# Input projections by Strassen block products over pairs of 512-token blocks, context tokens apart

## The chip, the cores and the metric

The kernel runs on one core of a Trainium2 chip. The metric is the device time of one execution, in microseconds (us); lower is better. Engines are named as in the profile: PE multiplies matrices (PEld is its weight load, which overlaps it), DVE, ACT and POOL work on vectors, SP only issues transfers. Work on one engine runs in the order in which it is written; between engines semaphores order it.

## The reference

One layer of a diffusion backbone: 2048 latent tokens of width 1024 and 256 context tokens.

```python
hx = modulate(rmsnorm(x, g_norm1[l]), mx[0], mx[1])      # (2048, 1024)
hc = modulate(rmsnorm(ctx, g_norm1[l]), mc[0], mc[1])    # (256, 1024)
px = split(hx @ w_in[l], IN_SPLIT_IDX)    # q 512, k 128, v 128, hq 512, i 512, ff 512, fb 512, g 512
pc = split(hc @ w_in[l], IN_SPLIT_IDX)
...
att_x = latent_attention(qx, kx, vx, kc, vc)             # softmax, 8 query heads, 2 key heads
hg_x, hg_c = hgrn2_bidirectional(px[3:], pc[3:], ...)    # gated recurrence over hq, i, ff/fb, g
x = x + mx[2] * (concat([att_x, hg_x]) @ w_out[l])
x = x + mx[5] * swiglu(modulate(rmsnorm(x, g_norm2[l]), mx[3], mx[4]), w_gu[l], w_down[l])
```

The change concerns the products of `hx` and `hc` with `w_in`. Of the context tokens only k, v, i and the two f are needed. All of it is float32.

## The kernel before

Float32 products are made of rounded parts: a factor is split into a high part (an ACT copy into a type with fewer bits) and a low part (the exact rest, one subtraction), and a product is high x high + high x low + low x high. So each product is three matmuls per 128 rows of the inner dimension.

The stages of the core's span, in order: an opening that loads the first columns of `w_mod` and the first tokens; normalisation, transposition and splitting of the tokens into `hT[b]` (block 0 is the context, blocks 1 to 4 are 512 latent tokens each), beside which PE already runs `jobs_kv` and the first half of hq; then the input projections, one after the other: q, the second half of hq, g, f and i; then attention and recurrence, the output projection, and the feed-forward part, which already uses Strassen's seven products.

The stretch that the change rewrites is q to i. A step is 256 columns of `w_in`, loaded into `wst` (1 MB), split by `split_w` (ACT copy L218, four DVE subtractions of 128x512 at L221) one step ahead into one of two homes, and then used for all tokens:
- "rows" jobs (`jobs_q`, `jobs_g`, `jobs_i`, by `mm_rows`, L442 and L448) give a tile of 128 tokens by 256 columns: for each of the 8 slices of 128 of the inner dimension a matmul of 512 columns (high tokens against high and low weights side by side) and one of 256 (low tokens against high weights). `both` (L453, L454) adds the two halves of the PSUM bank;
- "cols" jobs (`jobs_hq`, `jobs_f`, by `mm_cols`, L435) give a tile of 128 columns by 512 tokens (256 for the context): 24 matmuls, weights stationary.

The context's share of f and i is the first tiles of their steps. Behind the tiles, `pump` advances generators of side work: `qk_side` (normalisation and rotation of q and k, which are written to DRAM and read again; its transpositions are PE's), `mod_chunk` (16 products with further columns of `w_mod`, on DVE, L415 and L417) and, in the last step, `first_maxima` (the first row maxima of attention). PE's order here is written by hand; the order on the other engines is set by a list scheduler that knows a cost for each instruction, and SP issues nearly all transfers in one order too.

Of the kernel before, what the change touches and what calls it, by code (L numbers as in the profile page):

```python
# [9 lines left out]
F32 = mybir.dt.float32  # L10
# [57 lines left out]
def block_kernel(ctx: ExitStack, tc: tile.TileContext, a: dict, out: bass.AP, dbg=None):  # L68
# [24 lines left out]
    s_m0 = dram("s_m0", [4, P])  # L93
    s_att = [dram(f"s_att{j}", [256, T]) for j in range(2)]
# [79 lines left out]
    def load_tokens(gr, home, sp):  # L174
# [3 lines left out]
        for j in range(2):  # L178
            xt = home.tile([P, D], F32, tag="xt", name=f"xt{gr}_{j}")
            last_x[0] = nc.sync.dma_start(xt, src[j * P:(j + 1) * P, :])  # L180
            jk = xp2.tile([P, D], F32, tag="jk", name=f"jk{gr}_{j}") if gr else None
            xs.append((xt, jk))
# [21 lines left out]
    def load_raw(i, pieces):  # L204

        ws = wst_p.tile([P, KT, 256], F32, tag="wst", name=f"ws{i}")
# [7 lines left out]
    def split_w(i, ws, wp):  # L214

        whl = wp.tile([P, KT, 2, 256], F32R, tag="wh", name=f"wh{i}")
        wh, wl = whl[:, :, 0, :], whl[:, :, 1, :]
        nc.scalar.activation(wh, ws, AF.Copy)  # L218
        for q in range(4):
            ks = slice(2 * q, 2 * q + 2)  # L220
            (nc.vector if q % 2 or i > 1 else nc.gpsimd).tensor_tensor(  # L221
                wl[:, ks, :], ws[:, ks, :], f32v(wh[:, ks, :]), op=ALU.subtract)
        return wh, wl, whl
# [85 lines left out]
    with proj as st:  # L309
        w_pools = [w_left, w_right]  # L310
        hTp = pool(st, "hT")
        ev = pool(st, "ev", NEV)
        sm = pool(st, "sm", 4)
        sizes = [256, 512, 512, 512, 512]
        hT = [None] * 5
        for b in (4, 3, 1, 2):
            hT[b] = [hTp.tile([P, KT, sizes[b]], F32R, name=f"hT{w}{b}") for w in "hl"]
        ps_mm = pool(st, "ps_mm", 4, PSUM)
        nchunk = [1]
        turned = [None]  # L320

        def load_w(pieces):
# [3 lines left out]
            return split_w(i, load_raw(i, pieces), w_pools[i % 2])  # L326

        first = [early_w]
        with ExitStack() as p1:
            ps_x = pool(p1, "ps_x", 4, PSUM)  # L330
            xh = pool(p1, "xh", 3)
            for gr in list(range(1, NTOK // 256)) + [0]:
                if gr == 0:
                    xp.close()
                    hTc = pool(st, "hTc", side="right")
                    hT[0] = [hTc.tile([P, KT, 256], F32R, name=f"hT{w}0") for w in "hl"]
                    xp2 = pool(p1, "xp3", 2, side="right")
# [6 lines left out]
                with behind:  # L344
                    if gr == 1:
                        xs = early_x
                    else:
                        xs = ahead if gr == 2 else load_tokens(gr, xpp if gr else xp2, sm)
                        if gr == 0:
                            xs = [(xt, hT[0][1][:, 4 * j:4 * j + 4, :].rearrange("p k t -> p (k t)"))  # L350
                                  for j, (xt, _) in enumerate(xs)]
# [27 lines left out]
                def split_h(kk, hv, eng):  # L379

                    hi = hT[b][0][:, 2 * kk:2 * kk + 2, o:o + 256]
                    hd = nc.scalar.activation(hi, hv, AF.Copy)
                    return hd, eng.tensor_tensor(hT[b][1][:, 2 * kk:2 * kk + 2, o:o + 256], hv, f32v(hi), op=ALU.subtract)
# [11 lines left out]

        evF = pool(st, "evF", 1, side="right")
        qp = pool(st, "qp", 1, side="right")
        ps_t = pool(st, "ps_t", 2, PSUM)
        ps_q = pool(st, "ps_q", 2, PSUM)
# [30 lines left out]
        def mm_cols(pm, w, b, c0):  # L430

            n = sizes[b]
            for k in range(KT):
                for i, (wi, hi) in enumerate(((0, 0), (0, 1), (1, 0))):
                    nc.tensor.matmul(pm[:, :n], w[wi][:, k, c0:c0 + P], hT[b][hi][:, k, :],  # L435
                                     start=(k == 0 and i == 0), stop=(k == KT - 1 and i == 2))

        def mm_rows(pm, w, b, j, t=None):

            js = slice(j * P, (j + 1) * P)  # L440
            for k in range(KT):
                first = nc.tensor.matmul(pm, hT[b][0][:, k, js], w[2][:, k, :, :].rearrange("p w c -> p (w c)"),  # L442
# [1763 lines left out]
```

## Time and profile before

| | |
|---|---|
| median of 3 runs | 3110.43 us (3109.83 to 3116.51) |
| profiled execution | 3117.9 us, of it span 3116.1 us |
| granted clock | 0.996 |
| opening | 0 to 41 us |
| tokens, kv, first half of hq | 41 to 152 us |
| q, second half of hq | 152 to 292 us |
| g, f, i | 292 to 710 us |
| attention, recurrence, output projection | 710 to 1823 us |
| feed-forward | 1823 to 3116 us |

The stage borders are the first and last starts of each tile's matmuls in the trace. Tables by window give, for a stretch of the span, how long each engine was busy in it, with the number of its instructions in brackets; the timeline gives single instructions with their start, their length, and the idle time ahead of them with what ended it. The length of a matmul in the timeline includes its way through the pipeline; the rate is the distance between starts.

### The profile page before, as it was taken

The numbers are of one execution on the slowest core, as the hardware profiler recorded it, in microseconds if no ns is written. First come the engines' busy times: TensorE is split into PE (matmuls) and PEld (weight loads), VectorE is DVE, ScalarE is ACT, GpSimd is POOL, SyncE is SP. The second block draws the span as 40 slices with busy tenths as digits, with TensorE's granted clock in tenths as the row PEclk, the third lists the DMA queues.
The fourth block names the chain that finished last, engine by engine and source line by source line (L and its number), as shares of the span: only waits on it lengthen the run. The fifth ranks groups of instructions, "written<-read, shape, count | busy, mean of one in ns | idle before, by whom it ended". The sixth has DMA issues, their size and how long they took to land.

```text
span 3116.1 us, 51235 instructions
## 1 busy us (share of the span) xinstructions
PE 3074.8 (99%) x18844; PEld 2483.8 (80%) x18844; DVE 1845.9 (59%) x3252; ACT 1303.1 (42%) x2656; POOL 1602.7 (51%) x1291
## 2 busy tenths in 40 slices
PE   9999999999999999999999999999999999999999
PEld 7888888886777778777778878788888788888887
DVE  4554655427777787786745574544478743333567
ACT  4422322214545545555553253333345533333454
POOL 3311212106989888898862118676600277776122
PEclk9999999999999999999999999999999999999999
DMA  7544544425111212111124444656596533333765
GB/s 244 159 139 127 155 139 150 141 69 138 42 38 49 67 53 71 39 52 48 42 83 147 129 142 155 213 176 211 171 331 196 182 118 106 102 102 102 254 195 196
DMA packets 372998, 410.77 MB, mean 132 GB/s; under 512 B 34469, under 2 KB 264073, under 8 KB 372234
## 3 DMA queue, kind: packets, MB, share of 16 engines
q1 hardware_dynamic: 369722, 405.06, 41.0%
q8 instruction: 148, 2.42, 0.3%
q10 hardware_dynamic: 3024, 2.43, 0.2%
q14 instruction: 104, 0.85, 0.1%
HBM read 277.54 MB, written 133.97 MB: 132 GB/s over the span
## 4 chain that ended last, share of the span: by engine, by line
PE 70%; DVE 7%; DMA 5%; POOL 3%; issue 2%; ACT 1%; SPq 1%; POOLq 0%; DVEq 0%; ACTq 0%
PE pA L1785 13%; PE av L1215 7%; PE pB L1785 6%; PE y L1355 6%; PE pd0A L2082 4%; PE pd1A L2082 3%; PE s L1190 3%; PE s L1191 3%; PE pC L1785 3%; PE mx L1159 3%; PE i L442 2%; DVE mn L1161 2%; PE pd0B L2082 2%; PE pd1B L2082 2%; PE pa L818 2%
## 5 line engine op out<-in xcount | busy, mean ns | idle before, releaser
L1194 ACT ACTIVATE p<-s 128x512 f32<-128x512 f32 x576 | 338.2, 600 | 372.6 <-PE s L1191 358.1
L1161 DVE TENSOR_REDUCE mn<-mx 128x1 f32<-128x512 f32 x496 | 337.0, 689 | 175.2 <-PE mx L1159 172.3
L1215 PE MATMUL av<-p,VS 128*64 128x256 f32 x2304 | 259.9, 379 | 0.0
L1190 PE MATMUL s<-qa,K 128*128 128x512 f32 x576 | 244.1, 424 | 1.2 <-ACT p L1194 1.0
L1191 PE MATMUL s<-qb,KB 128*128 128x512 f32 x576 | 226.9, 394 | 0.0
L1215 PEld LDWEIGHTS av<-p,VS 128*64 128x64 f32 x2304 | 160.4, 137 | 75.3 <-issue 1.1
L1205 POOL TENSOR_TENSOR ps<-p,p 128x1024 f32<-128x1024 f32 x64 | 153.4, 2396 | 101.8 <-ACT p L1194 101.7
L1159 PE MATMUL mx<-K,qa 128*128 128x512 f32 x496 | 200.1, 404 | 2.4 <-DVE mn L1161 1.2
L435 PE MATMUL f<-hTh,wh 128*128 128x512 f32 (+1 forms) x640 | 188.1, 373 | 0.2 <-ACT ft L475 0.2
L1205 POOL TENSOR_TENSOR ps<-ps,p 128x1024 f32<-128x1024 f32 x64 | 153.1, 2392 | 12.0 <-ACT p L1194 10.6
L2019 DVE TENSOR_TENSOR dl<-dl,x 128x512 fp32r<-128x512 f32 x154 | 113.8, 765 | 66.5 <-ACT x L2012 64.9
L2012 ACT ACTIVATE x<-dl 128x512 fp32r<-128x512 f32 x154 | 95.9, 631 | 95.4 <-DMA dl<-s_hid0S 37.7
L852 POOL TENSOR_TENSOR Q<-Q,T 128x512 f32<-128x512 f32 x96 | 131.3, 1383 | 8.1 <-PE pa L818 7.7
L435 PEld LDWEIGHTS f<-hTh,wh 128*128 128x128 f32 x640 | 116.9, 190 | 20.4 <-ACT ft L475 0.3
L1190 PEld LDWEIGHTS s<-qa,K 128*128 128x128 f32 x576 | 109.0, 189 | 27.0 <-issue 12.3
L2012 ACT ACTIVATE dh<-dl 128x512 fp32r<-128x512 f32 x154 | 88.9, 624 | 98.7 <-PE pd1A L2082 42.2
L2019 DVE TENSOR_TENSOR dl<-dl,dh 128x512 fp32r<-128x512 f32 x154 | 105.5, 697 | 39.9 <-ACT dh L2012 37.7
L1159 PEld LDWEIGHTS mx<-K,qa 128*128 128x128 f32 x496 | 93.6, 189 | 38.0 <-DVE mn L1161 15.3
L131 POOL TENSOR_TENSOR rs_xf<-ms_xf,mhalf 128x1 f32<-128x1 f32 x16 | 9.9, 620 | 221.1 <-DVE ms_xf L129 218.5
L1191 PEld LDWEIGHTS s<-qb,KB 128*128 128x128 f32 x576 | 109.3, 190 | 14.9
L435 PE MATMUL f<-hTl,wh 128*128 128x512 f32 (+1 forms) x320 | 118.7, 371 | 0.0
L131 POOL TENSOR_TENSOR rs_qq<-ms_qq,mhalf 128x4 f32<-128x4 f32 x32 | 34.0, 1061 | 161.0 <-DVE ms_qq L129 160.3
(436 smaller groups left out, 8913.5 us busy)
## 6 DMA issues: line engine op xcount, KB each, us to landing
w<-in_w_gu_dram SPq DMA_DIRECT2D x88, 512.0 KB
wm<-in_w_mod_dram SPq DMA_DIRECT2D x24, 1024.0 KB
dl<-s_wT SPq DMA_DIRECT2D x88, 256.0 KB
dl<-s_wB SPq DMA_DIRECT2D x66, 256.0 KB
wq<-in_w_down_dram SPq DMA_DIRECT2D x44, 256.0 KB
s_wT<-wq SPq DMA_DIRECT2D x44, 256.0 KB
dl<-s_hid1S SPq DMA_DIRECT2D x44, 256.0 KB
dl<-s_hid0S SPq DMA_DIRECT2D x44, 256.0 KB
```

The source lines that it names most:

```text
L435: nc.tensor.matmul(pm[:, :n], w[wi][:, k, c0:c0 + P], hT[b][hi][:, k, :], start=(k == 0 and i == 0), stop=(k == KT - 1 and i == 2))
L1159: nc.tensor.matmul(s, self.qa[:, h * P:(h + 1) * P], K[:, k * 512:(k + 1) * 512], start=True, stop=True)
L1161: nc.vector.tensor_reduce(self.mn[:, h, k:k + 1], s, axis=AX.X, op=ALU.min)
L1190: nc.tensor.matmul(s, KS[self.g][:, ks], self.qa, start=True, stop=False)
L1191: nc.tensor.matmul(s, KB[k // 6][:, k % 6 * P:(k % 6 + 1) * P], self.qb, start=False, stop=True)
L1194: nc.scalar.activation(self.pairs[p][:, o:o + 512], s, AF.Exp, scale=-1.0)
L1205: (nc.gpsimd if SUMS[p] in "PQ" else nc.vector).tensor_tensor(t, a, self.pairs[p], op=ALU.add)
L1215: nc.tensor.matmul(self.av[i * 64:(i + 1) * 64, :256], VS[k // 6][:, k % 6, :], self.pairs[k // 2][:, o:o + 256], start=(k == 0), stop=(k ...
L1355: nc.tensor.matmul(py, m[:, k, :], wo[k][w][hf], start=(k == 0 and i == 0), stop=(k == KT - 1 and i == 2), skip_group_check=True)
L1785: nc.tensor.matmul(acc, w[wi][:, k, :], x[xi][k], start=(start and k == 0 and i == 0), stop=(stop and k == KH - 1 and i == 2), skip_group_ ...
L2019: nc.vector.tensor_tensor(lo, f32v(lo), f32v(hi), op=ALU.subtract)
L2082: nc.tensor.matmul(cur[t], l[:, t * P:(t + 1) * P], r, start=(start and j == 0 and f == 0), stop=(stop and j == NHF - 1 and f == 2), skip_ ...
```

## The change

The latent tokens' q, g, i, f and second half of hq are now made by Strassen's method in its seven-product form. The four 512-token blocks form two pairs; a pair's tokens (1024 x 1024) are taken as two blocks by two halves of the inner dimension (B11, B21, B12, B22), a chunk's weights as two groups of columns by the same halves. One chunk takes the place of two steps for half of the tokens: there are twelve, six for each pair (q; second half of hq with f of head 0; f of head 3, half as large; f of heads 1 and 2; g; i). Each of a chunk's seven phases multiplies one weight factor by one token factor, of half the inner dimension, into one of the accumulations A, C, B. The sums of token blocks T1 to T4 are made once per pair (`factors`), the sums of weights S1 to S4 in each chunk (`prepare`, called three phases ahead of their use).

```diff
+    s_tok = {n: [dram(f"s_t{n}{w}", [P, KT // 2, 512]) for w in "hl"] for n in ("B11", "B12", "B21", "B22")}
...
                 if gr == 0:
-                    xp.close()
+                    for n, at in (("B11", (1, 0)), ("B21", (1, 1)), ("B12", (2, 0)), ("B22", (2, 1))):
+                        for w in range(2):
+                            nc.sync.dma_start(s_tok[n][w], f32v(hT[at][w]))
...
+        queue = [(context_f, h, pieces_f(h)) for h in range(NH)] + \
+                [(context_i, c, [(C_I + c * 256, 256)]) for c in range(2)]
...
+        halves = [(slice(0, 2), nc.vector), (slice(2, 4), nc.gpsimd)]
+        def summed(x, first_term, *terms):
+            for ks, eng in halves:
+                acc = first_term[:, ks]
+                for op, t in terms:
+                    eng.tensor_tensor(x[:, ks], acc, t[:, ks], op=op)
+                    acc = x[:, ks]
+        def exact(name, x):
+            v = V[name] = quarter(name, f"v{name}")
+            for ks, _ in halves:
+                nc.scalar.activation(v[0][:, ks], x[:, ks], AF.Copy)
+            for ks, _ in halves:
+                nc.vector.tensor_tensor(v[1][:, ks], x[:, ks], f32v(v[0][:, ks]), op=MINUS)
+        def factors(place):
+            ...
+            summed(x, b12[0], (MINUS, b11[0]), (PLUS, b12[1]), (MINUS, b11[1]))
+            exact("T1", x)
+            summed(x, b22[0], (MINUS, x), (PLUS, b22[1]))
+            exact("T2", x)
+            summed(x, x, (MINUS, b11[0]), (MINUS, b11[1]))
+            exact("T3", x)
+            ...
+            summed(x, b21[0], (MINUS, t2[0]), (PLUS, b21[1]), (MINUS, t2[1]))
+            exact("T4", x)
+        def fetch_tokens(n, place):
+            V[n] = quarter(place, f"v{n}")
+            for w in range(2):
+                nc.sync.dma_start(f32v(V[n][w]), s_tok[n][w])
...
+        phases = [("A11", "B11", "A", True, False), ("A12", "B21", "C", True, True), ("S1", "T1", "B", True, False),
+                  ("S2", "T2", "A", False, False), ("S4", "B22", "B", False, True), ("S3", "T3", "A", False, False),
+                  ("A22", "T4", "A", False, True)]
+        def prepare(j):
+            ...
+            if name in sums:
+                x, y, o, op = sums[name]
+                src = wsum[:, o, :, :n]
+                nc.gpsimd.tensor_tensor(src, part(x), part(y), op=op)
+            else:
+                src = raw(name[1:])
+            t = W[j] = pl.tile([P, H, 2, 256], F32R, tag=tag, name=f"ws{j}")
+            nc.scalar.activation(t[:, :, 0, :n], src, AF.Copy)
+            nc.vector.tensor_tensor(t[:, :, 1, :n], src, f32v(t[:, :, 0, :n]), op=MINUS)
+            if m == 5: raws.pop((c, 0)); load_half(c + 1, 0)
+            if m == 6: raws.pop((c, 1)); load_half(c + 1, 1)
...
+        for c, (pair, ch) in enumerate(chunks):
+            turning = c == len(chunks) // 2 - 1
+            for m, (_, _, bk, start, _) in enumerate(phases):
+                for u in range(units):
+                    products(j, u, acc, ch)      # rows: 24 matmuls of 256 columns; cols: 12 of 512
+                    if m == 0: nc.scalar.activation(s0[u], acc, AF.Copy)
+                    elif m == 1: nc.vector.tensor_tensor(s0[u], acc, s0[u], op=ALU.add)
+                    ...
+                    pump(PUMP)
+                prepare(j + 3)
+                if turning:
+                    if m in fetches: fetch_tokens(fetches[m], PLACE[fetches[m]])
+                    if m == 4: made = factors("Xh")
+                    if m >= 5: next(made); next(made)
+                elif c == len(chunks) // 2:
+                    if m < 4: next(made, 0)
```

Beside this, the context's share of f and i stands ahead of the chunks, between the end of kv and the first chunk; the tokens of the second pair to be multiplied (blocks 1 and 2) go to DRAM (`s_tok`, 8 MB as high and low parts) and are fetched in chunk 5; the multiplication by `g_hg` goes from DVE to POOL; most stores of results go from SP's queue to ACT's; the PSUM banks of the q and k transpositions and of `mod_chunk` are shared; and the 16 `mod_chunk` follow one another without pause.

On PE, a step of q before; `q0_2` is the accumulation of one tile of 128 tokens, `hTh` and `hTl` the high and low tokens:

```order
L435 MATMUL hq041_1622<-hTh4_420,wh1_565 128x512
L442 MATMUL q0_2_1655<-wh2_1585,hTh1_424 128x512
L448 MATMUL q0_2_1655<-wh2_1585,hTl1_425 128x256
L442 MATMUL q0_3_1676<-wh2_1585,hTh1_424 128x512
L448 MATMUL q0_3_1676<-wh2_1585,hTl1_425 128x256
```

and the same place now, where `ws0` to `ws2` are the weight factors of phases 0 to 2 and `pA`, `pC`, `pB` the accumulations:

```order
L369 MATMUL i1_1_2153<-wh7_1_2040,hT0l_1090 128x256
L869 MATMUL pA0_0_2210<-ws0_2200,hT30h_441 128x256 x2
L869 MATMUL pA0_0_2210<-ws0_2200,hT30l_442 128x256
L869 MATMUL pA0_1_2211<-ws0_2200,hT30h_441 128x256 x2
L869 MATMUL pC0_0_2301<-ws1_2203,hT31h_431 128x256 x2
L869 MATMUL pC0_1_2302<-ws1_2203,hT31h_431 128x256 x2
L605 MATMUL pkNone_3_2364<-identr_120,skNone_3_2285 128x128 x2
L869 MATMUL pB0_0_2376<-ws2_2207,vT1h_1826 128x256 x2
```

Pairs of 512 and 256 columns have become triples of 256 columns, and a phase of 48 of them needs its own weight factor and token factor; the first chunk's follow the context's i (`i1_1`).

On DVE, between the last phases of chunk 5 (`pA5`) and phase 3 of chunk 6 (whose weight factor is `ws45`), eleven of the rows that now stand there, in their order; `sumXh` is the running sum of the token factors, `vT1l` to `vT4l` their low parts, `macc17` a product of `mod_chunk` and `sq1_12` a tile of the q side:

```order
L922 TENSOR_TENSOR rx_2192<-pA5_1_4440,rx_2192 128x512
L811 TENSOR_TENSOR ws43_4954<-wr60_4695,ws43_4954 128x4x256
L701 TENSOR_TENSOR sumXh_4957<-vB22h_4868,sumXh_4957 128x1024
L811 TENSOR_TENSOR ws44_5044<-wsum_2188,ws44_5044 128x4x256
L710 TENSOR_TENSOR vT3l_5210<-sumXh_4957,vT3h_5209 128x1024
L701 TENSOR_TENSOR sumXh_4957<-vB21h_4614,vT2h_5051 128x1024
L497 SCALAR_TENSOR_TENSOR macc17_4898<-wm17_4851,sc_144,macc17_4898 128x256
L583 TENSOR_TENSOR sq1_12_5040<-eq1_12_4861,sq1_12_5040 128x256
L701 TENSOR_TENSOR sumXh_4957<-sumXh_4957,vB21l_4615 128x1024
L710 TENSOR_TENSOR vT4l_5359<-sumXh_4957,vT4h_5358 128x1024
L811 TENSOR_TENSOR ws45_5134<-wsum_2188,ws45_5134 128x4x256
```

where before, in the middle of a step of g, DVE had only small work between two tiles:

```order
L454 TENSOR_TENSOR ge0_5_3194<-ge0_5_3194,g0_5_3177 128x256
L509 TENSOR_TENSOR ge0_5_3194<-ge0_5_3194,ghg_995 128x256
L557 TENSOR_TENSOR eq0_2_3415<-eq0_2_3415,rs_qq0_2_3455 128x256
L558 TENSOR_TENSOR eq0_2_3415<-eq0_2_3415,gqk_997 128x256
L454 TENSOR_TENSOR ge0_6_3239<-ge0_6_3239,g0_6_3222 128x256
```

Counted over the whole order, 17 of the 18 instructions of 128x1024 that make the second pair's factors stand ahead of `ws45` on DVE, and 13 of them, with the subtractions for `ws43` and `ws44`, ahead of the last row of `macc17`. PE reads these rows while it is in chunk 6, in this order (`pm17` is the matmul that sums `macc17` over the partitions, `pq1_12` the transposition of `sq1_12`):

```order
L869 MATMUL pA6_0_5057<-ws42_4865,vB11h_4522 128x256 x2
L502 MATMUL pm17_5084<-macc17_4898,ones_142 1x256
L869 MATMUL pA6_1_5058<-ws42_4865,vB11h_4522 128x256 x2
L590 MATMUL pq1_12_5118<-identr_120,sq1_12_5040 128x128 x4
L869 MATMUL pC6_0_5141<-ws43_4954,vB21h_4614 128x256 x2
L869 MATMUL pB6_0_5215<-ws44_5044,vT1h_4964 128x256 x2
L869 MATMUL pA6_0_5057<-ws45_5134,vT2h_5051 128x256 x2
```

So `pm17`, in the middle of phase 0 of chunk 6, stands behind most of the factor work of DVE.

On POOL, the same place has the other half of the sums, in one line with the sums of weights (`wsum`):

```order
L701 TENSOR_TENSOR sumXh_4957<-vB12h_4698,vB11h_4522 128x1024
L805 TENSOR_TENSOR wsum_2188<-wr61_4783 128x1024
L805 TENSOR_TENSOR wsum_2188<-wsum_2188,wr60_4695 128x1024
L701 TENSOR_TENSOR sumXh_4957<-vB22h_4868,sumXh_4957 128x1024
L805 TENSOR_TENSOR wsum_2188<-wr60_4695,wsum_2188 128x1024
L701 TENSOR_TENSOR sumXh_4957<-vB21h_4614,vT2h_5051 128x1024
L701 TENSOR_TENSOR sumXh_4957<-sumXh_4957,vT2l_5052 128x1024
L805 TENSOR_TENSOR wsum_2188<-wr60_4695,wr61_4783 128x1024
```

Before, POOL had there only the rotation's products and powers of the side work; now a weight sum can stand behind token sums.

461 lines of the change are left out of this document (309 added, 152 removed).

## The prediction

> **What bounds the kernel now.** First the page's line of busy times, then the table by window over the stages from q to i (us; busy time of each engine, granted clock, share of the DMA engines, GB/s), then what PE waits for in that stretch (total, times, longest).
>
> ```profile
> PE 3074.8 (99%) x18844; PEld 2483.8 (80%) x18844; DVE 1845.9 (59%) x3252; ACT 1303.1 (42%) x2656; POOL 1602.7 (51%) x1291
> core 0: us, PE busy (x) PEld busy (x) DVE busy (x) ACT busy (x) POOL busy (x), PEclk, DMA share, GB/s
> 152.20:245.80 93.60, 93.60 (x538) 80.03 (x537) 51.55 (x183) 24.01 (x65) 15.66 (x22) 1.00 0.46 141
> 245.80:291.70 45.90, 45.90 (x206) 36.73 (x205) 15.45 (x55) 10.27 (x28) 5.13 (x8) 1.00 0.37 116
> 291.70:386.30 94.60, 94.60 (x553) 81.49 (x552) 65.34 (x204) 37.28 (x96) 18.43 (x21) 1.00 0.48 143
> 386.30:603.70 217.40, 214.90 (x1075) 176.08 (x1073) 118.85 (x352) 59.97 (x117) 47.33 (x46) 0.99 0.49 149
> 603.70:709.60 105.90, 105.90 (x607) 92.25 (x607) 29.66 (x63) 18.28 (x43) 6.19 (x14) 1.00 0.30 94
> PE pq L584 <- ACT sq L585: 2.4, 1, 2.4
> ```
>
> The five windows are 557.4 us long and PE is busy for 554.9 of them at full clock. DVE works half of the time, POOL a sixth. So PE's matmuls are the time here: taking them away shortens the kernel one for one, until another engine, a transfer or a wait in PE's own order ends later.
>
> **What the change removes from PE.** The rate of a matmul is the distance between starts, read in the timeline (start, length, instruction):
>
> ```profile
> 386.54 0.40 PE L435 MATMUL f<-hTh,wh 128*128 128x256 f32 x2
> ...
> 390.13 0.40 PE L435 MATMUL f<-hTh,wh 128*128 128x256 f32 x2
> 604.07 0.28 PE L448 MATMUL i<-wh,hTl 128*128 128x256 f32 x1
> ...
> 607.60 0.28 PE L448 MATMUL i<-wh,hTl 128*128 128x256 f32 x1
> 246.34 0.63 PE L435 MATMUL hq<-hTh,wh 128*128 128x512 f32 x2
> ...
> 251.81 0.62 PE L435 MATMUL hq<-hTh,wh 128*128 128x512 f32 x2
> ```
>
> The first two rows are ten triples of 256 columns apart: 3.59/30 = 0.120 us a matmul. The next two are ten pairs of 512 and 256 columns apart, 0.353 us a pair. The last two are 24 matmuls of 512 columns apart, 0.228 us each.
>
> Rows: q, g and i of the latent tokens are six steps of 16 tiles of 8 pairs, 768 pairs x 0.353 = 271.1 us. They become six chunks x 7 phases x 48 = 2016 matmuls of 256 columns, 241.3 us: 29.8 less. A pair covers three blocks of 256 columns in 0.353 where three separate matmuls cost 0.359, so the split into 256 columns costs next to nothing, and 7/8 of the work remains. Cols: second half of hq and f are 192 + 768 = 960 matmuls of 512 columns, 218.8 us; four chunks of 168 and two of 84 are 840, 191.5 us: 27.3 less. The context's share keeps its matmuls, only earlier. Side work keeps its own (transpositions and sums, the 557.4 less some 525 of matmuls). Sum: **-57 us**.
>
> **What it adds, and what hides it.** Prices (line, operation, count, busy us, mean ns; the first row is a timeline row of four at once):
>
> ```profile
> 143.82 2.50 DVE L221 TENSOR_TENSOR wh<-ws,wh 128x512 fp32r<-128x512 f32 x4 [1.38 <-ACT wh L218]
> L1205 POOL TENSOR_TENSOR ps<-p,p 128x1024 f32<-128x1024 f32 x64 | 153.4, 2396 | 101.8 <-ACT p L1194 101.7
> L218 ACT ACTIVATE wh<-ws 128x2048 fp32r<-128x2048 f32 x13 | 24.8, 1910 | 4.8 <-DMA ws<-in_w_in_dram 4.8
> L1904 DVE TENSOR_TENSOR r<-pB,r 128x512 f32<-128x512 f32 x42 | 28.8, 686 | 34.5 <-PE pB L1785 32.3 <-issue 2.2
> L454 DVE TENSOR_TENSOR qe<-qe,q 128x256 f32<-128x256 f32 x32 | 13.2, 416 | 9.6 <-ACT qe L453 9.3
> 1880.00:2240.00 360.00, 357.89 (x1577) 295.37 (x1576) 170.63 (x191) 131.95 (x228) 259.62 (x189) 1.00 0.59 194
> L417 DVE SCALAR_TENSOR_TENSOR macc<-wm,sc,macc 128x256 f32<-128x256 f32 x112 | 53.9, 481 | 1.5
> 100.00:120.00 20.00, 20.00 (x115) 17.39 (x115) 12.37 (x23) 11.49 (x25) 10.20 (x10) 1.00 0.79 241
> 120.00:141.80 21.80, 21.80 (x119) 18.74 (x118) 2.30 (x6) 2.79 (x8) 0.00 (x0) 1.00 0.19 58
> 30.00:40.00 10.00, 10.00 (x94) 7.09 (x93) 3.44 (x16) 1.00 (x3) 0.00 (x0) 1.00 1.07 373
> 709.45 0.64 PE L1159 MATMUL mx<-K,qa 128*128 128x512 f32 x2
> 716.78 0.63 PE L1190 MATMUL s<-qa,K 128*128 128x512 f32 x1
> ```
>
> So 1024 columns cost DVE 1.25 us, POOL 2.40 and ACT 0.96 (half of 1.91); an addition out of PSUM of 512 columns costs DVE 0.69, which replaces the additions of 0.42.
>
> An ordinary chunk takes PE 40 us (rows: 336 x 0.120) or 38 (cols: 168 x 0.228). In it stand on DVE seven weight subtractions (8.8 us), six additions (4.1) and the side work it has now, 18 to 34 us in all; on POOL four weight sums, 9.6 us. A factor is prepared three phases ahead; after the phase that frees its slot, 11.5 us are left for copy and subtraction, 2.2. The feed-forward part works this way already, and its window (the row 1880 to 2240) shows PE busy in 357.9 of 360 us with POOL at 72%. I cost the eight ordinary chunks at 4 us together, between 0 and 12 (that window's loss of 0.6%, and a wait of one POOL instruction in half of the chunks). In the two small chunks a phase is only 2.7 us, and the adder of one phase gates the next but one: two waits of about an addition with its copy, 4 us, between 0 and 10.
>
> Start of chunk 0: a weight sum waits there until the context's i has left the slot, with three 2.40 us sums of T4 around it on POOL: 5 us, between 0 (they fit under 11.5) and 12. The other sums of the first set lie in the stretch of kv, where DVE was busy for 2.3 of 21.8 us (the row 120 to 141.8), and of the context's f and i, 34 us of PE.
>
> Stores of 8 MB ahead of the last token loads, on SP's queue: at the 373 GB/s of the row 30 to 40, 22 us of transfer, in a stretch whose DMA share was 0.79 at most (the row 100 to 120). PE has kv and hq to do meanwhile: 2 us, between 0 and 6. End: the result of `first_maxima` is now stored behind the last matmul; attention starts with 7 us of maxima that don't need it (709.45 to 716.78). They need K, whose load (1.2 MB, 3.2 us at that rate) waits for a weight slot that comes free one phase, 5.8 us, before the end: 3 us, between 0 and 6. The `g_hg` products on POOL and the stores on ACT's queue have idle time beside them: 0, unless POOL is late.
>
> **The turn.** This is the place on which the size rests. Let 0 be the end of phase 4 of chunk 5. PE has phases 5 and 6 and half a phase of chunk 6 to do, 2.5 x 5.76 = 14.4 us, then it wants `pm17`, whose `macc17` DVE finishes only behind 13 of the 18 factor instructions. Ahead of it from 0 on DVE has those 13 and three weight subtractions (16 x 1.25 = 20 us), the eight of `mod_chunk` (8 x 0.48 = 3.9), two additions (1.4) and the q side's small ones (some 4.5): 30 us, and some 1.5 of waiting for the additions' phases. So even if nothing else is in the way, PE waits about 17 us. Behind that `ws45` is 11.5 us of PE later and 9 us of DVE later: no second wait. The 8 MB of fetches (22 us at 373 GB/s, over five phases of 29 with 2 to 3 MB more) just fit.
>
> POOL makes the other halves: eight sums of 2.40 (19.2 us) must be done by then. Whether they run beside DVE's is shown by two places later in the span:
>
> ```profile
> 1157.90 5.89 DVE L1205 TENSOR_TENSOR ps<-ps,p 128x1024 f32<-128x1024 f32 x1
> 1157.58 0.46 POOL L855 TENSOR_TENSOR C<-M,T 128x128 f32<-128x128 f32 x1
> 1158.00 1.31 POOL L847 TENSOR_TENSOR M<-M,T 128x256 f32<-128x256 f32 x2
> 1159.27 2.17 POOL L852 TENSOR_TENSOR Q<-Q,T 128x512 f32<-128x512 f32 x2
> 1161.39 1.31 POOL L855 TENSOR_TENSOR C<-M,T 128x256 f32<-128x256 f32 x2
> 2048.95 1.61 DVE L1962 TENSOR_TENSOR wq<-wq,wq 128x512 f32<-128x512 f32 x1
> 2050.59 1.67 DVE L1964 TENSOR_TENSOR wq<-wq,wq 128x512 f32<-128x512 f32 x1
> 2048.27 1.74 POOL L1755 TENSOR_TENSOR A22l<-w,A22h 128x512 fp32r<-128x512 f32 x1
> 2049.97 1.74 POOL L1914 TENSOR_TENSOR r<-r,r 128x512 f32<-128x512 f32 x1
> ```
>
> A DVE addition of two SBUF tiles takes 5.89 us and ends only when POOL's unbroken row has ended at 1162.7; at 2049 the two engines take turns, and 0.63 us of DVE's work (2.50/4) spreads over 1.6. If all took turns here, DVE would be done at 20 + 3.6 (two-input rows of the q side) + 19.2 + 2.3 = 45 us: a wait of 31. Part of POOL's sums start before 0, and `mod_chunk` and the additions run beside POOL. Bounds 17 and 34; I take 26, nearer to turns, since both places show them.
>
> The Trainium skill, "SBUF — State Buffer", section "SBUF: two separate sides", says the same more strictly: a port pair is locked for a whole instruction, and a DVE instruction with two SBUF inputs and a POOL instruction that reads SBUF exclude each other. By that rule the wait is the 31 of full turns, and the sum is 5 us less of a gain. The trace agrees as far as the 5.89 us row goes.
>
> Sum of what is added: 26 + 4 + 4 + 5 + 2 + 3 = 44 us. **Net -57 + 44 = -13 us.** The profiled execution, 3117.9 us (span 3116.1 and 1.8 around it), was 7.5 above the median of the runs, so it would become 3105; against the median 3110.4 I predict 3097.
>
> **Rivals.** (1) All hidden but the turn's bare queue: POOL does not hold DVE up, the turn costs 17, all else 5: 57 - 22 = 35 us gained, 3075. For it: the feed-forward window; against it: the row of 5.89 us. (2) Slower: DVE and POOL exclude each other in every chunk. Chunks with 24 us of two-input DVE work and 10 to 13 of POOL then carry 37 of 38 to 40 us, so each late instruction makes a matmul of the side work wait, as `pq` did once above; 5 us in each of nine chunks instead of 4 in all, with a turn of 34 and 14 for the rest, are 93: 3146 at most, 3123 with half of the chunks. It decides from 64 us of waits on. Against it: the feed-forward window, where DVE works 171 and POOL 260 of 360 us and PE loses 2. (3) The fetches land late: they share the queue with weights and `mod_chunk`'s 1 MB loads; six more us for each of two fetches that gate T1 and T2, 12 us: 3109, no change. (4) Matmuls of 256 columns run at the duration of a weight load, 0.19 us, for 2016 x 0.07 = 141 us more:
>
> ```profile
> L435 PEld LDWEIGHTS f<-hTh,wh 128*128 128x128 f32 x640 | 116.9, 190 | 20.4 <-ACT ft L475 0.3
> ```
>
> The 128 x 256 rows of f above, 0.120 apart with a load for each matmul (the page counts as many of one as of the other), exclude it.
>
> **Numbers.** Forecast (3084 to 3104) 0.42; rival 1 and between (below 3084) 0.24; rival 3 (3104 to 3117) 0.17; rival 2 (above) 0.17. A change under 0.2%, 6.2 us, can't be told from none here. So faster 0.66, same 0.17, slower 0.17. The range leaves out the best tenth of rival 1 and the worst half of rival 2: 3066 to 3122.
>
> **What would show it.** PE's large matmuls from q to i rise from 2496 to 2856 with 57 us less between first and last start, beside the waits; one large PE gap at `pm17` in chunk 6, released by DVE L497 and 17 to 34 us long, with DVE's L701 and L710 rows stretched beyond 1.25 us; gaps under 2 us elsewhere. Wrong: if the gap is under 10 us (POOL and DVE overlap, or the order differs), if several chunks show gaps at `ws` rows, or if the largest gap is released by a transfer.

## The result and the profile after

The changed kernel takes 3187.05 us (median of 4 runs, 3181.97 to 3190.07) against 3113.34 us before (four runs, taken together with it): ratio 1.0235, 95% interval 1.0214 to 1.0257. That is 74 us slower; 3097 with a range up to 3122 was forecast. The profiled execution has a span of 3182.6 us, 66.5 longer.

The page's first part of the changed kernel: PE has 25 us less to do and the span is longer, so PE's share has fallen from 99 to 96%.

```profile
PE 3049.5 (96%) x19204; PEld 2490.3 (78%) x19204; DVE 2067.6 (65%) x3290; ACT 1396.2 (44%) x2718; POOL 1809.2 (57%) x1375
```

Windows of the changed kernel (busy us of PE, PEld, DVE, ACT, POOL; then granted clock, DMA share, GB/s), for the context stretch and the twelve chunks:

```profile
158.00:194.00 36.00, 35.50 (x264) 33.61 (x262) 24.52 (x64) 19.76 (x34) 5.34 (x6) 1.00 0.62 202
194.00:780.50 586.50, 494.06 (x3067) 438.08 (x3067) 447.89 (x823) 219.34 (x370) 271.02 (x181) 0.92 0.48 154
```

PE stands still for 92 of the 586 us of the chunks and its mean clock is 0.92; before, it stood still for 2.5 of 557 and the clock was 0.99 to 1.00. What PE waited for in the chunks (total, times, longest):

```profile
PE pm L502 <- DVE macc L497: 26.2, 1, 26.2
PE pA L876 <- DVE rx L922: 25.3, 6, 6.1
PE pA L869 <- DVE rx L922: 13.7, 4, 10.4
PE pA L876 <- ACT ft L512: 8.6, 4, 3.0
PE pC L869 <- DVE ws L811: 7.6, 1, 7.6
PE pA L869 <- ACT rx L828: 3.6, 1, 3.6
PE pA L869 <- ACT ft L512: 3.2, 2, 2.0
```

The first row is the turn, and so is the 10.4 us of the third. Otherwise rows two and three are one wait in most chunks (ten of twelve): phase 6 accumulates into bank A, which DVE's addition behind phase 5 (L922) must first have read. The ACT rows are the same at the seam of two chunks: phase 0 wants bank A while ACT still reads phase 6 out of it. Such a place in PE's timeline (chunk 1), and the clock behind it in windows of 2 us:

```profile
286.40 0.39 PE L876 MATMUL pA<-vT3h,ws 128*128 128x512 f32 x1
292.90 0.77 PE L876 MATMUL pA<-vT4h,ws 128*128 128x512 f32 x1 [6.11 <-DVE rx L922]
293.46 0.63 PE L876 MATMUL pA<-vT4l,ws 128*128 128x512 f32 x1
293.89 1.06 PE L876 MATMUL pA<-vT4h,ws 128*128 128x512 f32 x2
294.74 0.63 PE L876 MATMUL pA<-vT4l,ws 128*128 128x512 f32 x1
...
299.39 0.62 PE L876 MATMUL pA<-vT4h,ws 128*128 128x512 f32 x2
299.84 0.39 PE L876 MATMUL pA<-vT4l,ws 128*128 128x512 f32 x1
```

```profile
288.00:290.00 2.00, 0.00 (x0) 0.00 (x0) 2.00 (x3) 1.61 (x2) 1.92 (x2) 1.00 0.41 150
292.00:294.00 2.00, 1.10 (x3) 0.94 (x4) 2.00 (x9) 1.21 (x3) 1.17 (x2) 0.50 0.11 33
296.00:298.00 2.00, 2.00 (x6) 1.60 (x5) 1.27 (x4) 0.39 (x2) 0.47 (x1) 0.50 0.46 110
298.00:300.00 2.00, 2.00 (x9) 1.62 (x9) 1.08 (x6) 0.00 (x0) 0.68 (x2) 0.92 0.81 215
```

Behind the pause three matmuls take 1.28 us (293.46 to 294.74), 0.43 each, instead of 0.23 (two from 299.39 to 299.84), for some 5 us: the granted clock is 0.50 there. And what DVE did while PE waited for L922:

```profile
286.99 0.68 DVE L919 TENSOR_TENSOR rx<-pB,rx 128x512 f32<-128x512 f32 x1
287.59 0.28 DVE L564 TENSOR_TENSOR ekNone<-ekNone,gqk 128x128 f32<-128x128 f32 x1
287.79 0.28 DVE L563 TENSOR_TENSOR ekNone<-ekNone,rs_qkNone 128x128 f32<-128x128 f32 x1
287.99 1.49 DVE L497 SCALAR_TENSOR_TENSOR macc<-wm,sc,macc 128x256 f32<-128x256 f32 x1
289.40 1.74 DVE L811 TENSOR_TENSOR ws<-wr,ws 128x512 fp32r<-128x512 f32 x1
291.07 0.48 DVE L573 TENSOR_TENSOR ekNone<-ekNone,cskNone 128x32 f32<-128x32 f32 x4
291.48 0.28 DVE L564 TENSOR_TENSOR ekNone<-ekNone,gqk 128x128 f32<-128x128 f32 x1
291.68 0.47 DVE L497 SCALAR_TENSOR_TENSOR macc<-wm,sc,macc 128x256 f32<-128x256 f32 x1
292.08 0.68 DVE L922 TENSOR_TENSOR rx<-pA,rx 128x512 f32<-128x512 f32 x1
```

It was never idle: between the addition of phase 4 (L919) and that of phase 5 stand six rows of side work (`ekNone`, `macc`) and a weight split. Two of these rows are stretched: the `macc` row of 1.49 us takes 0.47 a little later, the split of 1.74 takes 0.69 in other places. The matmuls that the addition reads had all ended by 286.8.

**Where the 71 us went.** Attention starts at 780.6 instead of 709.45. Adding busy time x (1 - granted clock) over windows of 2 us gives what the clock costs: 26.8 us from 158 to 780, 1.6 before from 152 to 710. So: PE's work at full clock 553.9 to 502.8, -51; standing still 2.5 to 92.4, +90; clock +25; the stretch ahead of the context 152.3 to 158.0, +6. Sum +70. Behind that point the changed kernel is 4.6 us quicker (2402.0 against 2406.6 us to the end), which no run here explains.

### The profile page after: what moved, and what is told of

It reads as the page before. It is cut to its first block, busy times and chain, and to the rows that moved or that the text cites. A ratio compares the mean times of both kernels' runs of the same rounds, so it can differ in the third digit from the quotient of the medians.

```text
span 3182.6 us, 52050 instructions
## 1 busy us (share of the span) xinstructions
PE 3049.5 (96%) x19204; PEld 2490.3 (78%) x19204; DVE 2067.6 (65%) x3290; ACT 1396.2 (44%) x2718; POOL 1809.2 (57%) x1375
## 4 chain that ended last, share of the span: by engine, by line
PE 69%; DVE 6%; POOL 2%; DMA 2%; issue 1%; ACT 1%; SPq 0%; POOLq 0%; DVEq 0%; ACTq 0%
PE pA L2031 14%; PE av L1461 7%; PE pB L2031 7%; PE y L1601 5%; PE pd0A L2328 4%; PE pC L2031 3%; PE s L1436 3%; PE pd1A L2328 3%; PE s L1437 3%; PE mx L1405 3%; DVE mn L1407 2%; PE pd0B L2328 2%; PE pd1B L2328 2%; PE pa L1064 2%; PE av L1469 2%; PE pA L869 1%
## 5 line engine op out<-in xcount | busy, mean ns | idle before, releaser
L2295 POOL TENSOR_TENSOR y<-y,yg 128x512 f32<-128x512 f32 x24 | 40.5, 1705 | 144.8 <-DVE yg L2294 118.2
L1451 DVE TENSOR_TENSOR ps<-ps,p 128x1024 f32<-128x1024 f32 x64 | 111.4, 1741 | 6.2 <-POOL ps L1451 6.2
L2031 PE MATMUL pB<-x,S1h 128*128 128x512 f32 x352 | 109.7, 392 | 3.4 <-ACT S1h L2000 3.4
L2031 PE MATMUL pA<-x,S2h 128*128 128x512 f32 x352 | 110.5, 395 | 1.7 <-ACT S2h L2000 0.9
```

Of the source, the lines that this page charges most:

```text
L1451: (nc.gpsimd if SUMS[p] in "PQ" else nc.vector).tensor_tensor(t, a, self.pairs[p], op=ALU.add)
L2031: nc.tensor.matmul(acc, w[wi][:, k, :], x[xi][k], start=(start and k == 0 and i == 0), stop=(stop and k == KH - 1 and i == 2), skip_group_ ...
```

## The experiments

All ratios are against the kernel before, which ran beside them. The changed kernel stands at 1.0235 (1.0214 to 1.0257), so 0.002 of ratio is about what two of these can differ by without telling them apart.

**1. Loosen the bank of phase 6** (`e1_swap`): S3 ahead of S4, with the handlers and the sum's slot moved along.

```diff
-("S2", "T2", "A", ..), ("S4", "B22", "B", ..), ("S3", "T3", "A", ..), ("A22", "T4", "A", ..)
+("S2", "T2", "A", ..), ("S3", "T3", "A", ..), ("S4", "B22", "B", ..), ("A22", "T4", "A", ..)
```

> The phases S4 and S3 change places (A11, A12, S1, S2, S3, S4, A22), so that no phase accumulates into a bank right behind the phase whose DVE addition must still read it: phase 6 (A22 x T4) goes into bank A, and DVE's addition L922 reads bank A after S3 x T3. Theory BANK: the eight waits of phase 6 for L922, 38 us in all, and the half clock behind each (some 2 us) go: 45 to 55 us faster than the changed kernel, 3130 to 3142 us, with the gap at pm17 (26 us) still there. Rival LOAD: DVE has too much work in every chunk, and the waits come back at the next instruction of DVE that PE needs: at most 15 us faster, above 3170 us.

3184.23 us, ratio 1.0216 (1.0196 to 1.0237). L922 is gone from the list of waits, but PE now waits 24 us for ACT's sigmoids (L512) at the seam, 10 for ACT's copy L917 between S2 and S3, and 9 at transpositions. The bank named in the first list was where the lateness showed, not its only cause: theory BANK fell.

**2. Bank C first as well** (`e2_cfirst`):

```diff
-("A11", "B11", "A", ..), ("A12", "B21", "C", ..), ("S1", ..
+("A12", "B21", "C", ..), ("A11", "B11", "A", ..), ("S1", ..
```

> As e1_swap, and a chunk begins with A12 x B21 (bank C) ahead of A11 x B11 (bank A), so that the last phase of one chunk and the first of the next no longer use the same bank. Theory BANK: the seven waits of phase 0 for ACT's reading of bank A (15 us in all) go too, with 8 to 12 us of half clock: 15 to 25 us faster than e1_swap. Rival LOAD: no more than 5 us faster than e1_swap.

3195.4 us, 1.0251 (1.023 to 1.0272): 0.0035 above experiment 1, so no faster and rather slower. The waits for the sigmoids at the seam shrink from 24 to 3.6 us, those for the copy L917 grow from 11 to 21, and 25 us appear at the q side's transpositions (`pq`).

**3. All token sums on DVE** (`e3_alldve`):

```diff
-halves = [(slice(0, 2), nc.vector), (slice(2, 4), nc.gpsimd)]
+halves = [(slice(0, 2), nc.vector), (slice(2, 4), nc.vector)]
```

> Both halves of all sums of token factors on DVE; POOL has none of them. Theory LOCK (a DVE instruction with two SBUF inputs and a POOL instruction that reads SBUF exclude each other): ten sums of 2.4 us on POOL become ten of 1.2 on DVE, so the turn gets 8 to 12 us shorter (gap at pm17 14 to 18 us instead of 26), 3170 to 3182 us. Rival OVERLAP (POOL works beside DVE): DVE's queue gets 12 us longer ahead of pm17, the gap 34 to 38 us, 3192 to 3200 us.

3183.4 us, 1.0217 (1.0189 to 1.0246): neither. The turn's waits (from the end of chunk 5 to phase 0 of chunk 6) are 5.9 + 1.5 + 29.3 = 36.7 us against 10.4 + 26.2 = 36.6. DVE took over ten sums of 1.2 us and the turn did not get longer, so POOL's sums had cost it about as much: some 12 us, the half of the 24 that full turns would give. The rows agree roughly: taking the shortest tenth of each kind of row as its unhindered length, an estimate, DVE's rows at the turn are 17 us too long in the changed kernel and 7 here.

**4. No second set of factors** (`e4_nofact`): the `factors("Xh")` calls are left out, and the second pair is multiplied with the first pair's T1 to T4. The four fetches are kept, but that of B12 goes to other tiles (`Xh` instead of T1's home).

> Leaves out the 18 DVE and 10 POOL instructions that make the second pair's T1 to T4 (the first pair's are used again); the 8 MB of fetches stay. Both theories: the gap at pm17 (26 us and 2 of half clock) goes. Theory FACTORS: the 10.4 us wait at the end of chunk 5 goes too, 40 us faster in all, 3145 to 3150 us. Rival FETCH: that wait comes from the fetches (a store of the q side stands behind them in the queue, and ACT and DVE wait for it), so it stays at 8 to 11 us: 28 us faster, 3156 to 3162 us.

3152.99 us, 1.012 (1.0096 to 1.0144), 34 us faster than the changed kernel. The turn's waits fall from 36.6 to 4 us, the 10.4 at the end of chunk 5 with them, as FACTORS had it, though the total lies between the two forecasts. Since the fetch of B12 changed its place too, this run does not clear the fetches of the 10.4 (see below, the turn). The other waits stay (28 us for the addition behind phase 5 alone).

**5. No bank used twice within a phase and a half** (`e5_noadj`):

```diff
+phases: A11 (A), A12 (C), S2 (A), S1 (B), S3 (A), S4 (B), A22 (A)
+tag={"B": "b", "A": "ac"[c % 2], "C": "ca"[c % 2]}[bk]
```

> The phases in the order A11, A12, S2, S1, S3, S4, A22, and banks A and C change places from chunk to chunk, so that every reading of a bank by DVE or ACT has a phase and a half (8.6 us) before PE writes the bank again. Theory CHAIN (what costs is a reading that must end within 2.8 us while DVE and ACT work through their queues in order; e1_swap only moved such readings from DVE to ACT and to the next chunk's first phase): the waits for L922, L917, L512 and L828, 53 us in the changed kernel, fall below 12, with half of the half clock: 50 to 65 us faster than the changed kernel, 3122 to 3137 us. Rival LOAD (DVE is short of time in every chunk): the waits come back at the side work's transpositions and at the weights, as in e2_cfirst: at most 15 us faster.

3179.03 us, 1.0209 (1.0192 to 1.0226). LOAD was right: the waits at the banks fall from 54 to some 11 us, and instead PE waits 42 us at the transpositions of the q and k side. The waits of PE add up to 84 us (92 before the edit); those of the turn to 36.0, as in 1 (34), 3 and the changed kernel, though under other names each time. The two longest new rows:

```profile
PE pq L590 <- DVE sq L583: 18.7, 5, 8.1
PE pq L590 <- ACT sq L582: 17.1, 4, 9.0
```

**6. Also hold `mod_chunk` at the turn** (`e6_hold`):

```diff
+hold[0] = 2 if c > half + 1 else 1 if j < half * NP - 4 or j > half * NP + 5 else 0
 def pump(n):
-    if mqueue and next(mqueue[0], 0) == 0: mqueue.pop(0)
+    for _ in range(hold[0]):
+        if mqueue and next(mqueue[0], 0) == 0: mqueue.pop(0)
```

> As e5_noadj, and mod_chunk stands still from phase 3 of chunk 5 to phase 5 of chunk 6 and runs twice as fast from chunk 8 on, so that PE no longer meets pm17 in front of the factor work. Theory QUEUE: PE goes on to the next instruction that needs DVE (the transposition of sq1_12, then ws45), so of the 26 us 6 to 12 go: 6 to 12 us faster than e5_noadj. Rival: the wait is the factor work itself and only changes its name: within 4 us of e5_noadj.

3188.23 us, 1.0242 (1.0226 to 1.0257): 9 us slower than experiment 5, outside both forecasts. At the turn the rival was right: its waits are 36 us again, now at `pq` (19.6 the longest). The 9 us are another matter: the doubled rate later makes a new wait of 16.7 us at `pm`. So `pm17`, at which I had placed the turn's price, was only the first of several rows in line.

**7. `mod_chunk` without its arithmetic** (`e7_nomod`):

```diff
-nc.vector.tensor_scalar(acc, wm[:, 0, :], ..); 7 x nc.vector.scalar_tensor_tensor(..)
-nc.tensor.matmul(pm[:1, :256], ones, acc, ..); nc.vector.tensor_tensor(row, row, pm[:1, :256], ..)
```

> The changed kernel with mod_chunk reduced to its transfers: its 9 instructions of 128x256 on DVE and its matmul are left out, so the second and later thirds of the modulation are wrong (only the bias). DVE has 59 us less to do between chunk 0 and chunk 9. Theory LOAD: the waits of phases 6 and 0 (53 us) fall by more than half and the gap at the turn by 6 to 10; with the clock 45 to 60 us faster, 3127 to 3142 us. Theory CHAIN: DVE's share falls from 76 to 66%, the readings are still late now and then: 15 to 30 us faster, 3157 to 3172 us.

3162.39 us, 1.0158 (1.0143 to 1.0174), 25 us faster: inside CHAIN's range. The waits at banks fall only from 54 to 46 us, those of the turn from 36.6 to 26. DVE's share falls to 71%, not to the 66 forecast: rows of 81 us were taken away, and DVE's busy time fell by 49.

**8. No side work in the chunks** (`e8_noside`): `pump` and `first_maxima` moved behind the last chunk.

> The changed kernel with the side work (k and q side, mod_chunk) not advanced inside the chunks but all behind the last one, with first_maxima behind that; the whole run is longer by that tail, and only the stretch of the chunks is compared (586 us from 194 to 780 in the changed kernel, 89 us of it waits of PE). Theory SIDE: the readings and splits are late because they stand in DVE's and ACT's queues behind side work that waits for its own transfers; without it the waits in the chunks fall to the turn and chunk 0, 25 to 40 us, and the half clock to 10: the chunks take 495 to 515 us. Rival BANK: the chunk's own chain of matmul, reading and weight split is too tight; waits stay above 60 us and the chunks take above 545 us.

The chunks take 472 us instead of 586 (one execution, as in 9 and 10). The window of that run, and then its list of waits of PE:

```profile
194.00:666.40 472.40, 444.19 (x2850) 406.65 (x2849) 245.91 (x243) 171.08 (x235) 185.47 (x84) 0.97 0.34 115
```

```profile
PE pC L869 <- DVE ws L811: 7.5, 1, 7.5
PE pA L869 <- DVE rx L916: 5.5, 2, 4.7
PE pA L869 <- ACT ft L512: 5.5, 2, 3.0
PE pB L869 <- DVE ws L811: 5.0, 3, 4.5
PE pA L876 <- ACT ft L512: 1.9, 2, 1.0
PE pA L876 <- DVE rx L916: 1.8, 2, 0.9
```

Of 114 us, PE's own side work (transpositions, `pm`) is 32; 64 are waits and 18 clock. Even the turn falls to 10 us, and the waits at banks to 15 in all: the chunks with their tight banks are nearly fit to keep PE busy, as long as the side work is out of the way. Theory SIDE: its waits (25 to 40 us; 28 measured) and its clock (10; 9) came as forecast, and the length of the chunks was passed because the forecast left PE's own side work in. What the run does not tell is by which of its loads the side work does the harm, since DVE, ACT and POOL are all rid of it at once.

**9. The same with the loosened banks** (`e9_noside_noadj`).

> As e8_noside, with the phase order and bank exchange of e5_noadj. Theory SIDE: hardly a difference to e8_noside in the chunks (within 10 us), since nothing is late. Rival BANK: 20 us or more shorter than e8_noside.

The chunks end 5 us earlier (467 us). Without side work the banks hardly matter.

**10. Which side work** (`e13_modonly`): only the q and k side moved behind the chunks.

> As e8_noside, but mod_chunk keeps its place in the chunks; only the q and k side is moved behind them. Only the stretch of the chunks is compared: 586 us with all side work, 473 with none. If the q and k side with its chain over SP, ACT, DVE and POOL does the harm: 485 to 505 us. If it is the amount of DVE work (mod_chunk is 59 us of it, the q and k side some 95): 515 us or more.

514 us. One window for each, in this order: no `mod_chunk` (experiment 7), no q and k side (this one); with the rows above for all and none.

```profile
196.00:754.80 558.80, 482.64 (x3048) 437.08 (x3047) 398.51 (x680) 220.59 (x369) 266.00 (x179) 0.93 0.52 163
```

```profile
194.00:708.50 514.50, 461.50 (x2889) 412.01 (x2888) 317.31 (x380) 171.60 (x235) 183.79 (x94) 0.95 0.40 135
```

DVE is busy for 448, 399, 317 and 246 us of 586, 559, 514 and 472: 76, 71, 62 and 52%; PE stands still for 92, 76, 53 and 28 us. The waits fall with DVE's load, whichever part is taken away, and at 62% they are not gone. The 514 us lie between the two forecasts, 1 us from that for the amount of DVE work.

**11 and 12. Less side work on ACT** (`e11_noact`, and `e12_noadj_noact` with the banks of experiment 5): squares of q and k on POOL, their high parts on DVE.

```diff
-nc.scalar.activation(e[:, :n], raw, AF.Square)
+nc.gpsimd.tensor_tensor(e[:, :n], raw, raw, op=ALU.mult)
-nc.scalar.activation(sk[:, n:], e[:, :n], AF.Copy)
+nc.vector.tensor_copy(sk[:, n:], e[:, :n])
```

> The changed kernel with the side work of q and k taken off ACT as far as its head of line waits go: the squares on POOL, the high parts on DVE (ACT keeps only the copies of the transpositions). Theory HEAD (the side work does its harm where its instruction stands at the head of ACT's queue and waits for a load or for DVE, 41 + 41 + 22 + 18 us in the chunks, with splits and bank readings behind it): the waits of PE fall from 89 to 50 or less, 35 to 55 us faster than the changed kernel, 3132 to 3152 us. Rival SPREAD (the lateness is that of DVE and POOL as much): within 15 us of it, above 3170 us.

> Both e5_noadj and e11_noact. Theory HEAD: the bank readings have 8.6 us and the splits no longer wait behind loads, so what is left is the turn, chunk 0 and some transpositions: 55 to 75 us faster than the changed kernel, 3112 to 3132 us, about as fast as the kernel before. Rival SPREAD: as e5_noadj, 3170 to 3182 us.

3203.22 us, 1.0287 (1.0266 to 1.0307), and 3203.23 us, 1.0287 (1.0268 to 1.0305): both slower than the changed kernel by 16. DVE is busy for 469 us of the chunks in the first, 21 more, and PE stands still for 101 from 158 on. HEAD fell; the edit did more harm on DVE and POOL than it took away on ACT.

**13. Stores back on SP** (`e10_spst`): the three `nc.scalar.dma_start` of results made `nc.sync.dma_start`.

> The changed kernel with the stores of results issued by SP again instead of ACT. Theory ACTQ: ACT's queue holds the splits up while a store at its head waits for DVE; 10 to 20 us faster, 3167 to 3177 us. Rival: SP's queue is no shorter (it waits for POOL and DVE at every q tile), and loads of weights come later: same or up to 15 us slower.

3186.56 us, 1.023 (1.0213 to 1.0247): the same, as the rival had it. On the whole it costs nothing whose queue issues them. At the turn the 10.4 us wait is gone, but that at `pm17` is 33.2 us instead of 26.2.

**14 and 15. What a pause costs** (`g6_gaps`, `g2_gaps`): the kernel before with pauses of PE in f and i.

```diff
+nc.tensor.matmul(pg[:, :P], ident, ident, ..)
+for _ in range(k): nc.scalar.activation(pg[:, :P], pg[:, :P], AF.Copy)   # k = 16, and 4
+nc.scalar.activation(gap_t, pg[:, :1], AF.Copy)
+nc.tensor.matmul(pg[:1, :1], ones, gap_t, ..)
```

> The kernel before with twelve artificial pauses of PE in f and the first half of i: a small matmul, sixteen ACT copies in a chain (some 5.5 us) and a matmul that needs their end. Theory CLOCK: behind each pause PE runs at half clock for some 4.6 us and loses 2.3 us more, so twelve pauses cost 12 x (5.5 + 2.3) = 94 us, 3200 to 3215 us. Rival: the low clock in the changed kernel comes from something else (its mix of matmuls), and the pauses cost their own length: 66 us, 3172 to 3185 us.

> The kernel before with 24 short pauses of PE (four ACT copies in the chain, 1.3 to 3 us each) instead of twelve of 5 to 10. Theory THRESHOLD: a pause below some 2.5 us leaves the clock alone, and only the longer ones of these cost 2.2 us more; lost to the clock below 15 us, the rest is the pauses' own length. Rival: every pause costs the same 2.2 us of half clock, 53 us in all.

Twelve pauses: 3224.66 us, 1.0359 (1.0339 to 1.0379), 110 us slower. In the trace they are 81 us long together (5.0 to 9.9), and 28 us are lost to the clock against 1.6: 2.2 behind each. Theory CLOCK; its total was passed because the pauses were longer than meant. Twenty-four pauses: 3185.38 us, 1.0232 (1.0217 to 1.0248); 48 us of pauses, 11 lost to the clock. Single ones of the second kernel, each pause with a window of the 5 us behind it:

```profile
418.63 0.19 PE L616 MATMUL gq<-gt,ones 128*1 128x1 f32 x2 [1.91 <-ACT gt L614]
468.23 0.19 PE L616 MATMUL gq<-gt,ones 128*1 128x1 f32 x2 [2.22 <-ACT gt L614]
597.31 0.19 PE L616 MATMUL gq<-gt,ones 128*1 128x1 f32 x2 [2.44 <-ACT gt L614]
```

```profile
418.70:423.70 5.00, 5.00 (x19) 4.05 (x20) 0.59 (x2) 1.43 (x3) 0.54 (x1) 0.66 0.57 161
468.30:473.30 5.00, 5.00 (x26) 3.84 (x27) 0.56 (x2) 0.79 (x2) 0.00 (x0) 1.00 0.23 53
597.40:602.40 5.00, 5.00 (x20) 3.49 (x19) 0.41 (x1) 0.60 (x1) 0.00 (x0) 0.70 0.24 53
```

Behind 2.22 us the clock stays at 1.00; behind 1.91 and 2.44 it is 0.66 and 0.70. Of all 24, the three longer ones (2.44, 2.92 and one of 5.48) lowered the clock and the eight of 1.5 us did not; of the thirteen between 1.7 and 2.3 us four did (1.74, 1.88 and twice 1.91) and nine did not, 2.22 among them. The loss of the run is that of theory THRESHOLD, but the length of a pause alone does not tell whether it costs; the last section has what does.

## Why the prediction was wrong, step by step

- **The matmuls, -57: nearly right.** PE's work at full clock fell by 51. Where the other 6 are I can't say; the spacing of the new matmuls behind no pause is the 0.120 and 0.228 us assumed.
- **The ordinary chunks, "4 us together, between 0 and 12": the step that failed.** The eight lost some 30 us in waits, 19 at phase 6 and 11 at the seam; the two small chunks lost 12 where 4 stood in the sum. Three things were wrong in it. First, I looked only at the weight factor, which has 11.5 us, and not at the reading of a bank that the next phase writes, which has 2.7 to 2.9: a reader of the phase table sees S3 and A22 both on bank A, with DVE's addition between. Second, I took the feed-forward window as proof, but PE's order there is another. In all 18 cases of that window it works on two other accumulations between S3 and A22, for 5.2 us or more; one case, first rows only:

```profile
2027.35 0.62 PE L1785 MATMUL pA<-x,S3h 128*128 128x512 f32 x2
2028.03 0.62 PE L1785 MATMUL pC<-x,A12h 128*128 128x512 f32 x2
2030.75 0.62 PE L1785 MATMUL pB<-x,S1h 128*128 128x512 f32 x2
2033.24 0.62 PE L1785 MATMUL pA<-x,A22h 128*128 128x512 f32 x2
```

  There DVE is also less loaded (171 of 360 us, 47%, of it 42 side work of its own, `wq`), and some of the weight splits are POOL's. Third, the side work: without it the chunks lose 28 us in all, with it 92 (experiment 8), and loosening the banks alone gained 8 us (experiment 5). The row of DVE's share in an ordinary chunk, "18 to 34 us in all" of 38 to 40, stood in the prediction and was read as "fits"; a queue that is three quarters full and in order often needed more than 2.8 us to deliver.
- Before, the same side work ran beside these stages (DVE 281 of 557 us in all) and ACT waited for its loads as long (64.6 us for `s_qraw` before, 41.8 in the chunks), yet harmlessly: tiles went through four PSUM banks in turn, 2.8 to 5.4 us each, and a weight step had 45 us of lead. The change spent that slack and raised DVE's busy time to 448 of 586 us. No run tells the two apart.
- **The clock: a term that was missing.** 25 us. The page's clock of 0.996 and the window's 0.99 of f before were the one hint, and I read "full clock" out of them. A wait that I priced at its length costs some 2 us more as soon as it lowers the clock (2.2 in experiment 14).
- **The turn, 26 us at `pm17` behind DVE L497: the place was right, the size by luck.** The gap is 26.25 us, but both times that it lies between were forecast 13 us too early. From the end of phase 4 (466.1) DVE needed 53.5 us to the last row of `macc17`, not 40.4, and PE needed 27.4 to `pm17`, not 14.4, with a wait of 10.4 us before phase 6 that the prediction did not have. So the turn cost 36.7 us, above its bound of 34, and experiments 1, 3, 5 and 6 show 34 to 37 under any name. DVE's 13 us have two parts. It stood still for some 9 us, most of them here:

```profile
472.80 0.42 ACT L582 ACTIVATE sq<-eq 128x256 fp32r<-128x256 f32 x1 [10.71 <-DMA vB12l<-s_tB12l]
473.25 1.75 DVE L583 TENSOR_TENSOR sq<-eq,sq 128x256 fp32r<-128x256 f32 x1 [9.27 <-ACT sq L582]
```

  ACT's next in line, a store of i (L836), was issued only at 472.31, when the fetch of `vB12l` had landed, with L582 behind it and DVE's queue behind that. So rival 3's late fetch had a hand in the 10.4 us; in experiment 13, with the stores off ACT's queue, that wait is gone and `pm17` waits longer instead. The other part is the stretch of DVE's rows beside POOL: 17 us by the estimate of experiment 3 (single rows of 1.2 us take 2.8 to 3.4), where the forecast of 26 held some 9. The sum had counted POOL's token sums alone, which experiment 3 puts at about 12 us; its weight sums stand there too. The Trainium skill, "SBUF — State Buffer", section "SBUF: two separate sides", has a DVE instruction with two SBUF inputs and a POOL instruction that reads SBUF exclude each other; the stretched rows agree with it.
- **Chunk 0, 5 us: 11** (7.6 and 0.9 for weight splits, 2.6 at phase 6). **Opening, 2 us: 6**, with 3.9 of it a wait of kv for DVE, which was busy for 19.8 of the 20 us from 120 to 140 with the first factors; I had counted that stretch as free room. **End, 3 us: 2.**
- **Rival 2** had the right sign, the right place, every chunk, and more of the mechanism than I gave it, though the measured time lies above its 3146 too. The weight subtractions show little of POOL's hold: 1.36 and 1.44 us in the mean instead of 1.25, some 10 us in 70. The side work's rows show more; an addition of the q side, first before, then now (32 times, 0.42 and 0.92 us in the mean):

```profile
L572 DVE TENSOR_TENSOR eq<-eq 128x256 f32<-128x256 f32 x32 | 13.5, 422 | 13.8 <-POOL eq L571 13.8
L578 DVE TENSOR_TENSOR eq<-eq 128x256 f32<-128x256 f32 x32 | 29.5, 924 | 8.3 <-POOL eq L577 8.3
```

  By the same estimate (shortest tenth of each kind as the unhindered length) 78 rows of DVE in the chunks are longer by over 0.2 us, by 106 us in all, and each of them lies beside a row of POOL, which is busy for 271 us here; before there were 9, by 3 us, beside 93 us of POOL. So a good part of DVE's rise from 281 to 448 us is this stretch. It is not enough by itself: in experiment 8 it is still 58 us, and PE waits for only 28. How much of PE's waits it makes stays open, since no run takes the weight sums off POOL. The rival's sentence that "each late instruction makes a matmul of the side work wait" is what experiments 2, 5 and 6 show.

What stays open: which part of the lateness comes from DVE's stretch beside POOL and which from the order in the queues (the list scheduler's, and the q side's chain over four engines and two transfers); why the waits grow as they do from 52 to 76% of DVE's load; and whether another order of the side work would do. No version here beats the kernel before.

## What to carry to other kernels

Before trading PE's matmuls for work on the other engines, write down for each thing PE needs how long the maker has, from input ready to PE's need, and what else stands in that maker's queue; a share of busy time that leaves room does not say that each piece comes in time. A stage that keeps PE busy elsewhere in the kernel is a proof only with the same order of banks and the same neighbours in the queues. A forecast of a gap as the difference of two times is borne out only when both times are: here both were 13 us off. When loosening one wait leaves the sum of the waits about as it was, as in experiments 1, 2, 5 and 6, the lateness is upstream: take work out of the queue instead.

## What the runs showed of the hardware

After PE has stood idle long enough, the granted clock is 0.50 and matmuls of 512 columns stand 0.43 us apart instead of 0.228 (changed kernel, 293.46 to 294.74 us). The twelve long pauses of experiment 14 cost 2.2 us each by it.

Where a pause lies counts beside its length. In the run with 24 pauses (experiment 15) the pieces at half clock are 3.4 us long (6.8 behind the pause of 5.48 us), and they begin at 399.0, 419.5, 484.4, 576.5, 597.0, 614.1 and 644.8 us, whole multiples of 3.41 us apart: the clock changes only on the borders of a fixed grid. Cutting the trace into these slots, every slot in which PE was idle for 1.74 us or more is followed by one at half clock, and in the stretch of the pauses none with up to 1.69 us is. The pauses of 1.74 to 1.91 us that lowered the clock lie wholly inside one slot; that of 2.22 us is cut by a border into 1.27 and 0.95 and costs nothing. From q to i the same cut gives a border near 1.7 to 1.9 us of idle time in the changed kernel, in experiment 5 and in experiment 12.

The Trainium skill, "TensorE: Matmul & The Clock Gate", section "HAM oscillation — how this bites in real kernels", warns of idle gaps above some 3.4 us. The mechanism agrees, the border does not: here half as much, if it fell into one slot, was enough.
